# The first input's parts made straight from PSUM, its squares summed as loaded, and a 128-byte buffer below the weights

## The chip, the cores and the metric

The kernel runs on one core of one Trainium2 chip. The metric is the time of one execution on the device in microseconds; before the change the median of three runs is 2146.05 us (2145.6 to 2146.09).

## The reference

Four layers over one sequence of 256 tokens with 1024 features, all in float32. Each layer adds half of a SwiGLU feed-forward network (FFN), a token mixer, and half of a second FFN:

```python
for layer in range(DEPTH):                                   # 4
    h = h + 0.5 * swiglu(rmsnorm(h, ffn_norm[layer, 0]), ffn_w_gate_up[layer, 0], ffn_w_down[layer, 0])
    hn = rmsnorm(h, mixer_norm[layer])                       # mixer: gated DeltaNet, short convolution,
    h = h + mix(hn)                                          # sparse attention, gated DeltaNet
    h = h + 0.5 * swiglu(rmsnorm(h, ffn_norm[layer, 1]), ffn_w_gate_up[layer, 1], ffn_w_down[layer, 1])
rmsnorm(x, w) = x * rsqrt(mean(x * x) + 1e-6) * w
swiglu(h, gu, dn): g, u = split(h @ gu); (silu(g) * u) @ dn   # 1024 -> 2 x 2816 -> 1024
```

## The kernel before

**Parts.** Every float32 operand of a large product is split in two: `hi`, the value rounded to the float32r format that TensorE (PE) takes, and `lo`, what the rounding left. A product is three matmuls, hi by hi, lo by hi and hi by lo (`mm3`, lines 335 to 337). The activations are kept transposed, features on partitions, and are the moving operand of 256 columns (`xhi`, `xlo`, and later `hhi`, `hlo`); a block of 128 by 128 of a weight's part is the stationary one. In a few places (the last down projection, `last_rows`, lines 418 to 420, and the `add_wide` pieces of the mixers, lines 1433 to 1435 and 1983 to 1986) it is the other way round: the weights' part moves with 512 columns.

**Weights.** `Weights` streams them through four `raw` buffers of 8 KB per partition. SP issues the loads. `hi()` makes a half buffer's high part on ScalarE (ACT) or VectorE (DVE), `lo()` the low part on DVE, into six buffers each of `whi` and `wlo` of 4 KB. Where a stage has room, parts go into lent `b8` buffers instead (`wboth`). A piece of 48 matmuls takes two halves.

**Addresses.** Buffers are stacked in each partition's memory in the order of their pools (const, big, work, raw, parts), at multiples of 32 bytes. In the built program all `b8` buffers (activations' parts and lent parts) begin at 224 modulo 256 bytes, and `raw`, `whi` and `wlo` at 160; rows and blocks inside them are whole multiples of 512 bytes long, so that every moving operand and stationary block named above begins at those residues too.

**The start.** x is loaded with tokens on partitions (`xin`), in two halves of 512 features, and then the first weights, of which the first `raw` buffer in quarters. PE transposes x into PSUM; DVE copies it to `x`, ACT makes `xhi` with the norm's weight as a scale, DVE makes `xlo`, POOL (GpSimd) squares it. The sums of the squares over the features are matmuls with one column (`norm_sums`, line 315). The first piece's matmuls are written so that parts which come late are used late (`first_cols`, `late_cols`). The row factor of the norm is only applied behind the products (`norm_rows`, `rb`). Fillers (`busy`) keep PE at work while it waits for x.

**Order.** Everything is issued in the order in which the code is written; a planner sets the order inside the mixers. Each engine takes its own instructions in that order and waits on semaphores.

Of the kernel before, what the change touches and what calls it, by code (L numbers as in the profile page):

```python
# [7 lines left out]
F32 = mybir.dt.float32  # L8
# [3 lines left out]
AF = mybir.ActivationFunctionType  # L12
OP = mybir.AluOpType
AX = mybir.AxisListType

D = 1024
S = 256
DFF = 2816
KT = D // 128
FT = DFF // 128  # L20
EPS = 1e-6
# [9 lines left out]
class Weights:  # L31
# [45 lines left out]
    def view(t, dims):  # L77
# [3 lines left out]
        names = "abc"[:len(dims)]  # L81
        return t[:, :n].rearrange(f"p ({' '.join(names)}) -> p {' '.join(names)}", **dict(zip(names, dims)))

    def load(self):
        while not self.hold and self.loaded < min(self.freed + self.LOADS, len(self.srcs)):
            src = self.srcs[self.loaded]
            raw = self.view(self.raw_pool.tile([128, 2048], F32, name="raw"), src.shape[1:])
            if len(src.shape) == 4:

                n = src.shape[3] // (1 if self.loaded else 2)  # L90
                for c in range(0, src.shape[3], n):
                    for b in range(src.shape[2]):
                        self.nc.sync.dma_start(raw[:, :, b, c:c + n], src[:, :, b, c:c + n])
            else:
                self.nc.sync.dma_start(raw, src)
            self.raw[self.loaded] = raw
            if self.plan:
                self.plan.set(("raw", self.loaded), 5.0)
            self.loaded += 1
# [72 lines left out]
def kernel(ctx, tc, plan, a, out):  # L172
    nc = tc.nc
# [3 lines left out]
    work = ctx.enter_context(tc.tile_pool(name="work", bufs=2))  # L177
    psum = ctx.enter_context(tc.tile_pool(name="psum", bufs=1, space=bass.MemoryType.PSUM))
    W = Weights(tc, ctx)

    def bank(tag="acc"):
        return psum.tile([128, 512], F32, name=tag, tag=tag, bufs=4)

    def mid():
        return bank("mid")

    def b8(dt, name, shape=(KT, S)):
        return big.tile([128, *shape], dt, name=name, tag="b8", bufs=10)
# [3 lines left out]
    def t2(name, shape=(2, S), dt=F32):  # L192
        return work.tile([128, *shape], dt, name=name, tag="t2", bufs=8)
# [35 lines left out]
    for kind, layer, i in plan:  # L229
        if kind == "ffn":  # L230
            steps.append((add_pairs(a["ffn_w_gate_up"][layer, i]), add_rows(a["ffn_w_down"][layer, i], DFF)))
        if kind == "gdn":
            w = a["gdn_w_in"][i]
            units = {}
            for u in GDN_ORDER:
                c = D * "qkvg".index(u[0]) + 512 * int(u[1])
                units[u] = (add_wide if u[0] == "g" else add_cols)(w, *([c] if u[0] == "g" else [c, 512]))
            steps.append((units, add_rows(a["gdn_w_out"][i], D)))
        if kind == "nsa":
            w = a["nsa_w_in"][i]  # L240
# [4 lines left out]
        if kind == "sc":  # L245
            w = a["sc_w_in"][i]
# [3 lines left out]
    xin = b8(F32, "xin", (2, D))  # L250
    norm_rows = t2("norm_rows", (128,))[:96]
    nc.sync.dma_start(norm_rows[:64], a["ffn_norm"].rearrange("l i (k p) -> (l i k) p", p=128))
    nc.scalar.dma_start(norm_rows[64:], a["mixer_norm"].rearrange("l (k p) -> (l k) p", p=128))
    for c in range(0, D, 512):
        nc.sync.dma_start(xin[:, :, c:c + 512], a["x"][0, :, c:c + 512].rearrange("(t p) d -> p t d", p=128))
    W.load()


    ij = const.tile([128, 128], I32, name="ij")
# [3 lines left out]
    ones = const.tile([128, 128], F32, name="ones")  # L263
# [1 line left out]
    neghalf = const.tile([128, 16], F32, name="neghalf")  # L265
    nc.vector.memset(neghalf, -0.5)

    def busy(times):

        p = mid()  # L270
        for _ in range(times):
            nc.tensor.matmul(p[:, :128], ones, ident, start=True, stop=True)


    x = const.tile([128, KT, S], F32, name="x")
    busy(5)
    p = bank()
    nc.tensor.transpose(p[:, :96], norm_rows, ident[:96, :96])
    norms = const.tile([128, 96], F32, name="norms")
    nc.vector.tensor_copy(norms, p[:, :96])  # L280

    class Normed:
        pass


    def norm_start():
        n = Normed()
        n.hi, n.lo = b8(F32R, "xhi"), b8(F32R, "xlo")
        n.sq = b8(F32, "sq")
        return n  # L290

    def norm_hi(n, k, col, squares=True):
        for kk in (k, k + 1):
            nc.scalar.activation(n.hi[:, kk], x[:, kk], AF.Copy, scale=norms[:, col + kk:col + kk + 1])  # L294
        if squares:
            norm_square(n, k)

    def norm_square(n, k):
        nc.scalar.activation(n.sq[:, k:k + 2], x[:, k:k + 2], AF.Square)

    def norm_lo(n, k, col):
        for kk in (k, k + 1):
            nc.vector.scalar_tensor_tensor(n.lo[:, kk], x[:, kk], norms[:, col + kk:col + kk + 1], n.hi[:, kk],
                                           op0=OP.mult, op1=OP.subtract)

    def norm_squares(n, k):

        nc.vector.tensor_add(n.sq[:, :2], n.sq[:, :2], n.sq[:, k:k + 2])

    def norm_sums(n):  # L310

        p = bank()
        for t in range(2):
            for k in range(2):
                nc.tensor.matmul(p[:, t:t + 1], n.sq[:, k, t * 128:(t + 1) * 128], ones[:, :1], start=k == 0,
                                 stop=k == 1)
        n.r = work.tile([128, 2], F32, name="rcol")
        yield
        nc.vector.tensor_scalar(n.r, p[:, :2], 1.0 / D, EPS, op0=OP.mult, op1=OP.add)  # L319
        yield  # L320
        nc.gpsimd.tensor_tensor(n.r, n.r, neghalf[:, :2], op=OP.pow)  # L321

    def norm_rows(n):

        dg = t2("dg", (2, 128))
        for t in range(2):
            nc.vector.tensor_scalar(dg[:, t], ident, n.r[:, t:t + 1], None, op0=OP.mult)
        p = bank()[:, :S]
        nc.tensor.matmul(p, ones, dg, start=True, stop=True)
        W.lo()  # L330
        n.rb = work.tile([128, S], F32, name="rb")
        nc.vector.tensor_copy(n.rb, p)
# [6 lines left out]
    def pair(tag="acc"):  # L339
        return bank(tag).rearrange("p (s t) -> p s t", s=2)  # L340

    def rest(steps):

        while True:
            try:
                next(steps)
            except StopIteration as end:
                return end.value

    def add_rows_steps(pieces, inputs, ktiles, scale, next_col, engine=None, planned=False):  # L350
# [3 lines left out]
        for q, j in enumerate(pieces):  # L354
# [3 lines left out]
            if last:  # L358
                nn = norm_start()
# [74 lines left out]
    def first_cols(j, acc, ks, n):  # L434

        parts = [[v.rearrange("p (s c) -> p s c", s=2) if len(v.shape) == 2 else v for v in W.part(j, k)] for k in ks]
        for k, (hi, lo) in zip(ks, parts):
            for s in range(2):
                for x in (n.hi, n.lo):
                    nc.tensor.matmul(acc[:, s], hi[:, s], x[:, k], start=k == 0 and s == 0 and x is n.hi, stop=False,  # L440
                                     skip_group_check=True)
        for k, (hi, lo) in zip(ks, parts):
            for s in range(2):
                nc.tensor.matmul(acc[:, s], lo[:, s], n.hi[:, k], start=False, stop=False, skip_group_check=True)

    def two_cols(j, acc, ks, n):

# [21 lines left out]
    def dense(j, n, first=False):  # L469
        acc = pair()  # L470
        W.use(j)
        if j == 0:
            first_cols(j, acc, range(4), n)
        else:
            (late_cols if first else two_cols)(j, acc, range(4), n)
        (late_cols if first else two_cols)(j, acc, range(4, KT), n)
        W.retire(j)
        return acc

    def two_first(pieces, n):  # L480

        accs = [dense(pieces[0], n, True), pair()]
        W.use(pieces[1])
        for k in range(KT):
            if k == 2:
                rest(norm_sums(n))
                W.hi()
                W.hi()
            if k == 5:
                norm_rows(n)  # L490
                W.ahead(pieces[0] + 3)
            two_cols(pieces[1], accs[1], [k], n)
        W.retire(pieces[1])
        W.ahead(pieces[1] + 3)
        return accs
# [1563 lines left out]
    cols = []  # L2059
    for kind, layer, i in plan:  # L2060
        cols.append((layer * 2 + i) * 8 if kind == "ffn" else 64 + layer * 8)
    cols.append(None)
    n = norm_start()
    busy(4)
    for k in range(0, KT, 2):
        if k == 4:
            busy(4)
        p = bank().rearrange("p (k t) -> p k t", k=2)
        for kk in range(2):
            for t in range(2):  # L2070
                nc.tensor.transpose(p[:, kk, t * 128:(t + 1) * 128],
                                    xin[:, t, (k + kk) * 128:(k + kk + 1) * 128], ident)
        nc.vector.tensor_copy(x[:, k:k + 2], p)
        norm_hi(n, k, cols[0], False)
        nc.gpsimd.tensor_mul(n.sq[:, k:k + 2], x[:, k:k + 2], x[:, k:k + 2])
        if k == 2:
            W.hi()
        if k:
            norm_lo(n, k - 2, cols[0])
        if k == 6:  # L2080
            W.lo()
    norm_lo(n, KT - 2, cols[0])
    W.ahead(0)
    W.hi()
    W.hi()
    W.lo()
    for k in range(2, KT, 2):
        norm_squares(n, k)
    W.ahead(1)
    def loads_of(kind, i):  # L2090
        return gdn_loads(g, i) if kind == "gdn" else nsa_loads(g, i) if kind == "nsa" else iter(())

# [2 lines left out]
    for q, (kind, layer, i) in enumerate(plan):  # L2095
        if kind == "ffn":
            then = (plan[q + 1:q + 2] or plan[:1])[0]
            n = ffn(steps[q], n, cols[q + 1], loads_of(then[0], then[2]), dict(gdn=SPARE, nsa=min(SPARE, 3)).get(then[0], 0))
        if kind == "gdn":
            n = gdn(steps[q], n, cols[q + 1], g)  # L2100
        if kind == "nsa":
            n = nsa(steps[q], n, cols[q + 1], g)
        if kind == "sc":
            n = sc(steps[q], n, cols[q + 1])
# [42 lines left out]
```

## Time and profile before

| | |
|---|---|
| median of three runs | 2146.05 us |
| the profiled execution | 2144.0 us, of which the span of its instructions 2142.2 us |
| PE busy | 2119.2 us, 99% |
| PE loading weights (PEld) | 2065.6 us, 96% |
| DVE, ACT, POOL busy | 66%, 50%, 13% |
| granted TensorE clock, mean | 0.998 of full |

Matmuls are pipelined and their recorded durations overlap, so that the pace of a stretch is read from the starts: the start of the last less that of the first, over the number of matmuls between them. In the names `out<-in`, `acc` and `mid` are PSUM banks. PE at the start, before about 28 us, is where it waits for others; behind that it is given work almost without a gap.

### The profile page before, as it was taken

How to read it: one execution, taken by the hardware profiler on the slowest of the kernel's cores; microseconds unless marked ns; L12 is line 12 of the kernel's file. 1: busy time of each engine (PE TensorE's matmuls, PEld its weight loads, DVE VectorE, ACT ScalarE, POOL GpSimd, SP SyncE). 2: the span in 40 equal slices, each digit the busy share in tenths (PEclk: the TensorE clock that was granted, in tenths of full speed). 3: DMA queues.
4: the chain of work that ended last, by engine and by line, in shares of the span. 5: the costliest groups of instructions: out<-in, count | busy, mean ns of one | idle time of the engine just before them, and what ended most of it. 6: DMA issues, size and time to landing. Idle time of an engine off the chain costs nothing. (4 is left out here: it accounts for less than half of the span.)

```text
span 2142.2 us, 41781 instructions
## 1 busy us (share of the span) xinstructions
PE 2119.2 (99%) x17335; PEld 2065.6 (96%) x17335; DVE 1407.0 (66%) x2322; ACT 1066.0 (50%) x1800; POOL 283.7 (13%) x312
## 2 busy tenths in 40 slices
PE   8999999999999999999999998999999999999999
PEld 8999999999999999999999987899999999999997
DVE  7664897665566476665666468876556648986653
ACT  5453754544454355444555445654445436655542
POOL 2110101121021010210121010011102201011210
PEclk9999999999999999999999999999999999999999
DMA  8564451556565555655566443155546562524652
GB/s 246 185 242 138 140 181 40 177 178 211 157 204 189 186 167 188 194 182 196 165 200 230 145 162 119 55 187 184 192 157 200 197 236 89 168 85 138 198 196 80
DMA packets 263790, 363.22 MB, mean 170 GB/s; under 512 B 17856, under 2 KB 211520, under 8 KB 263600
## 3 DMA queue, kind: packets, MB, share of 16 engines
q1 hardware_dynamic: 257520, 357.11, 50.6%
q8 instruction: 136, 2.23, 0.4%
q10 hardware_dynamic: 5136, 2.12, 0.4%
q0 software_dynamic: 944, 1.33, 0.3%
q14 instruction: 54, 0.44, 0.1%
HBM read 357.89 MB, written 2.10 MB: 168 GB/s over the span
## 5 line engine op out<-in xcount | busy, mean ns | idle before, releaser
L136 DVE TENSOR_TENSOR wlo<-raw,whi 128x1024 fp32r<-128x1024 f32 x640 | 775.4, 1219 | 234.6 <-ACT whi L126 234.2
L335 PE MATMUL acc<-xhi,whi 128*128 128x256 f32 x3248 | 911.7, 281 | 0.0
L337 PE MATMUL acc<-xhi,wlo 128*128 128x256 f32 x3248 | 909.1, 280 | 0.0
L336 PE MATMUL acc<-xlo,whi 128*128 128x256 f32 x3248 | 907.6, 279 | 0.0
L126 ACT ACTIVATE whi<-raw 128x1024 fp32r<-128x1024 f32 x633 | 660.2, 1050 | 352.1 <-PE mid L336 204.1
L336 PEld LDWEIGHTS acc<-xlo,whi 128*128 128x128 f32 x3248 | 610.7, 188 | 0.5
L337 PEld LDWEIGHTS acc<-xhi,wlo 128*128 128x128 f32 x3248 | 609.7, 188 | 0.0
L335 PEld LDWEIGHTS acc<-xhi,whi 128*128 128x128 f32 x3248 | 608.9, 187 | 0.5
L510 POOL TENSOR_TENSOR t_h<-t_gate,rb 128x256 f32<-128x256 f32 x176 | 197.8, 1124 | 740.9 <-ACT t_gate L506 735.7
L337 PE MATMUL mid<-hhi,wlo 128*128 128x256 f32 x1056 | 295.1, 279 | 0.0
L336 PE MATMUL mid<-hlo,whi 128*128 128x256 f32 x1056 | 294.4, 279 | 0.0
L335 PE MATMUL mid<-hhi,whi 128*128 128x256 f32 x1056 | 294.4, 279 | 0.0
L506 ACT ACTIVATE t_gate<-t_gate 128x256 f32<-128x256 f32 x176 | 73.6, 418 | 311.0 <-DVE t_gate L505 311.0
L505 DVE TENSOR_TENSOR t_gate<-acc,rb 128x256 f32<-128x256 f32 x176 | 74.5, 423 | 189.3 <-PE acc L337 189.3
L336 PEld LDWEIGHTS mid<-hlo,whi 128*128 128x128 f32 x1056 | 198.6, 188 | 0.0
L337 PEld LDWEIGHTS mid<-hhi,wlo 128*128 128x128 f32 x1056 | 198.3, 188 | 0.0
L335 PEld LDWEIGHTS mid<-hhi,whi 128*128 128x128 f32 x1056 | 197.9, 187 | 0.0
L512 DVE TENSOR_TENSOR t_h<-acc,t_h 128x256 f32<-128x256 f32 x176 | 74.8, 425 | 128.7 <-POOL t_h L510 128.7
L517 ACT ACTIVATE hhi<-t_h 128x256 fp32r<-128x256 f32 x176 | 73.7, 419 | 152.1 <-DVE t_h L512 152.1
L321 POOL TENSOR_TENSOR rcol<-rcol,neghalf 128x2 f32<-128x2 f32 x12 | 8.4, 704 | 654.4 <-DVE rcol L319 654.4
L519 DVE TENSOR_TENSOR hlo<-t_h,hhi 128x256 fp32r<-128x256 f32 x176 | 74.0, 420 | 7.7 <-ACT hhi L517 7.7
L294 ACT ACTIVATE xhi<-x,norms 128x256 fp32r<-128x256 f32 x96 | 43.2, 498 | 48.5 <-DVE x L368 42.2
(437 smaller groups left out, 2591.5 us busy)
## 6 DMA issues: line engine op xcount, KB each, us to landing
raw<-in_ffn_w_gate_up_dram SPq DMA_DIRECT2D x350, 512.0 KB, 5.3
raw<-in_ffn_w_down_dram SPq DMA_DIRECT2D x88, 1024.0 KB, 5.0
raw<-in_gdn_w_in_dram SPq DMA_DIRECT2D x32, 1024.0 KB, 5.4
raw<-in_nsa_w_in_dram SPq DMA_DIRECT2D x10, 1024.0 KB, 5.1
raw<-in_gdn_w_out_dram SPq DMA_DIRECT2D x8, 1024.0 KB, 5.1
raw<-in_sc_w_in_dram SPq DMA_DIRECT2D x16, 512.0 KB, 4.7
raw<-in_sc_w_in_dram SPq DMA_DIRECT2D x4, 1024.0 KB, 6.0
raw<-in_sc_w_out_dram SPq DMA_DIRECT2D x4, 1024.0 KB, 5.7
```

The source lines that it names most:

```text
L126: self.nc.scalar.activation(self.parts[g][0], raw, AF.Copy)
L136: (engine or self.nc.vector).tensor_sub(self.parts[g][1], self.half(g), self.parts[g][0])
L294: nc.scalar.activation(n.hi[:, kk], x[:, kk], AF.Copy, scale=norms[:, col + kk:col + kk + 1])
L335: nc.tensor.matmul(o, w[0], x[0], start=first, stop=False, skip_group_check=True)
L336: nc.tensor.matmul(o, w[0], x[1], start=False, stop=False, skip_group_check=True)
L337: nc.tensor.matmul(o, w[1], x[0], start=False, stop=last, skip_group_check=True)
L505: nc.vector.tensor_mul(t, acc[:, 0], n.rb)
L506: nc.scalar.activation(s, t, AF.Silu)
L510: nc.gpsimd.tensor_mul(sr, s, n.rb)
L512: nc.vector.tensor_mul(h, acc[:, 1], sr)
L517: nc.scalar.activation(hi, h, AF.Copy)
L519: nc.vector.tensor_sub(lo, h, hi)
```

## The change

The transposes of x now go to `mid` banks, and the parts are made straight from there: ACT makes `xhi` and DVE `xlo` from PSUM, without the copy to `x` before. The copies to `x` (needed for the residual) are made by ACT later, inside the second piece of the first FFN. The squares are taken of `xin` as it was loaded, tokens on partitions, by ACT, which adds them up along the features as it goes (`accum_out`); so the sum over features needs no matmul, only an addition of two halves on DVE. The `sq` buffer isn't used for the first norm. The two pairs of sums stand in a new buffer `xsums` of 2 x 16 float32 values, 128 bytes, in the pool that lies below `raw` and the parts: these now begin at 32 modulo 256 bytes instead of 160, everything in `big` stays at 224.

SP loads x and the first two `raw` buffers in another order: the quarter-columns that the first piece needs come first. The first `whi` is made on DVE. The first piece uses one order for both halves of the features: all hi by hi, all lo by hi, all hi by lo. The row factor is formed one step later (`k == 6`).

```diff
+    def first(self, inputs):
+        srcs = self.srcs[:2]
+        raw = [self.view(self.raw_pool.tile([128, 2048], F32, name="raw"), x.shape[1:]) for x in srcs]
+        n = srcs[0].shape[3] // 2
+        for c in range(2):
+            for x in range(2):
+                if c == 0:
+                    self.nc.sync.dma_start(*inputs[x])
+                for b in range(2):
+                    self.nc.sync.dma_start(raw[x][:, :, b, c * n:c * n + n], srcs[x][:, :, b, c * n:c * n + n])
...
     def norm_sums(n):
...
+            sums = n.r
         yield
-        nc.vector.tensor_scalar(n.r, p[:, :2], 1.0 / D, EPS, op0=OP.mult, op1=OP.add)
+        if n.sums:
+            nc.vector.tensor_add(n.r, *n.sums)
+        nc.vector.tensor_scalar(n.r, sums, 1.0 / D, EPS, op0=OP.mult, op1=OP.add)
...
     def first_cols(j, acc, ks, n):
...
+        for w, x in ((0, n.hi), (0, n.lo), (1, n.hi)):
+            for k, both in zip(ks, parts):
+                for s in range(2):
+                    nc.tensor.matmul(acc[:, s], both[w][:, s], x[:, k], start=k == 0 and s == 0 and not w and x is n.hi,
+                                     stop=w == 1 and k == KT - 1, skip_group_check=True)
...
             if k == 2:
-                rest(norm_sums(n))
+                if n.sums is None:
+                    rest(norm_sums(n))
                 W.hi()
                 W.hi()
-            if k == 5:
+                if n.sums:
+                    n.copies()
+            if k == (5 if n.sums is None else 6):
                 norm_rows(n)
...
-        nc.vector.tensor_copy(x[:, k:k + 2], p)
-        norm_hi(n, k, cols[0], False)
-        nc.gpsimd.tensor_mul(n.sq[:, k:k + 2], x[:, k:k + 2], x[:, k:k + 2])
...
+    sums = work.tile([128, 2, 16], F32, name="xsums", bufs=1)
+    n.sums = [sums[:, h, :2] for h in range(2)]
...
+        for kk in range(2):
+            c = cols[0] + k + kk
+            nc.scalar.activation(n.hi[:, k + kk], p[:, kk], AF.Copy, scale=norms[:, c:c + 1])
...
+            nc.vector.scalar_tensor_tensor(n.lo[:, k + kk], ps[k][:, kk], norms[:, c:c + 1], n.hi[:, k + kk],
+                                           op0=OP.mult, op1=OP.subtract)
...
+            nc.scalar.activation(t2("xsq"), xin[:, t, 512 * h:512 * h + 512].rearrange("p (k c) -> p k c", k=2),
+                                 AF.Square, accum_out=n.sums[h][:, t:t + 1])
...
+    busy(4, "acc")
+    ps = {k: turned(k) for k in (0, 2)}
+    W.hi("V")
+    remains(0)
+    remains(2)
+    W.lo()
+    square_sums(0)
+    W.hi()
+    busy(4, "acc")
+    for k in (4, 6):
+        ps[k] = turned(k)
+        remains(k)
+    W.lo()
     W.hi()
     W.hi()
+    square_sums(1)
     W.ahead(1)
+    rest(norm_sums(n))
+
+    def copies():
+        for k in ps:
+            nc.scalar.activation(x[:, k:k + 2], ps[k], AF.Copy)
```

How the instructions move, at three places of the start; the names are tiles, the figures partitions by elements, xN a run of equal ones. First the loads that SP issues, before:

```order
L252 DMA norm_rows<-in_ffn_norm_dram 64x128
L255 DMA xin<-in_x_dram 128x2x512 x2
L93 DMA raw<-in_ffn_w_gate_up_dram 128x4x128 x4
L93 DMA raw<-in_ffn_w_gate_up_dram 128x4x256 x42
L95 DMA raw<-in_ffn_w_down_dram 128x2x1024 x11
```

and now:

```order
L264 DMA norm_rows<-in_ffn_norm_dram 64x128
L92 DMA xin<-in_x_dram 128x2x512
L94 DMA raw<-in_ffn_w_gate_up_dram 128x4x128 x2
L92 DMA xin<-in_x_dram 128x2x512
L94 DMA raw<-in_ffn_w_gate_up_dram 128x4x128 x6
L105 DMA raw<-in_ffn_w_gate_up_dram 128x4x256 x40
```

Two quarter loads of weights stand ahead of the second half of x, and the second buffer's first quarters ahead of the first buffer's last ones.

Then ACT from its first table load to the first gate of the FFN, before:

```order
L294 ACT_TABLE_LOAD
L294 ACTIVATE xhi<-x,norms 128x256 x4
L126 ACTIVATE whi<-raw 128x1024
L294 ACTIVATE xhi<-x,norms 128x256 x4
L126 ACTIVATE whi<-raw 128x1024 x9
```

and now (`xsq` is a scratch buffer that nobody reads):

```order
L2094 ACT_TABLE_LOAD
L2094 ACTIVATE xhi<-mid,norms 128x256 x4
L2105 ACTIVATE xsq,xsums<-xin 128x512 x2
L138 ACTIVATE whi<-raw 128x1024
L2094 ACTIVATE xhi<-mid,norms 128x256 x4
L138 ACTIVATE whi<-raw 128x1024 x2
L2105 ACTIVATE xsq,xsums<-xin 128x512 x2
L138 ACTIVATE whi<-raw 128x1024 x2
L2129 ACTIVATE x<-mid 128x512 x4
L138 ACTIVATE whi<-raw 128x1024 x4
```

Squares and copies of x have come to ACT, and one whi has left it.

Last DVE, from the copy of the norms on, before:

```order
L280 COPY norms<-acc 128x96
L2073 COPY x<-acc 128x512 x2
L303 SCALAR_TENSOR_TENSOR xlo<-x,norms,xhi 128x256 x2
L2073 COPY x<-acc 128x512
L303 SCALAR_TENSOR_TENSOR xlo<-x,norms,xhi 128x256 x2
L2073 COPY x<-acc 128x512
L303 SCALAR_TENSOR_TENSOR xlo<-x,norms,xhi 128x256 x2
L136 TENSOR_TENSOR wlo<-raw,whi 128x1024
L303 SCALAR_TENSOR_TENSOR xlo<-x,norms,xhi 128x256 x2
L136 TENSOR_TENSOR wlo<-raw,whi 128x1024 x2
L308 TENSOR_TENSOR sq<-sq 128x512 x3
L136 TENSOR_TENSOR wlo<-raw,whi 128x1024
```

and now:

```order
L291 COPY norms<-acc 128x96
L140 CAST whi<-raw 128x1024
L2100 SCALAR_TENSOR_TENSOR xlo<-mid,norms,xhi 128x256 x4
L148 TENSOR_TENSOR wlo<-raw,whi 128x1024
L2100 SCALAR_TENSOR_TENSOR xlo<-mid,norms,xhi 128x256 x4
L148 TENSOR_TENSOR wlo<-raw,whi 128x1024 x3
L338 TENSOR_TENSOR rcol<-xsums 128x2
L339 TENSOR_SCALAR rcol<-rcol 128x2
```

The four copies and three additions are gone, the first whi is here, and the first wlo stands ahead of the second four remainders.

## Rows read from the trace of the kernel before

**Rows 1.** Page, part 1: busy time, share of the span and instructions of TensorE.
```profile
PE 2119.2 (99%) x17335; PEld 2065.6 (96%) x17335; DVE 1407.0 (66%) x2322; ACT 1066.0 (50%) x1800; POOL 283.7 (13%) x312
```

**Rows 2.** Groups by line, tile and shape, TensorE: count, busy us, mean ns, idle.
```profile
L335 PE MATMUL acc<-xhi,whi 128*128 128x256 f32 x3248 | 911.7, 281 | 0.0
...
L335 PE MATMUL mid<-hhi,whi 128*128 128x256 f32 x1056 | 294.4, 279 | 0.0
...
L465 PE MATMUL acc<-xhi,whi 128*128 128x256 f32 x168 | 42.8, 284 | 0.0
...
L335 PE MATMUL acc<-gzh,whi 128*128 128x256 f32 x128 | 36.3, 283 | 0.0
...
L418 PE MATMUL mid<-whi,hhi 128*128 128x512 f32 x88 | 34.7, 394 | 0.0
...
L1983 PE MATMUL acc<-whi,xhi 128*128 128x512 f32 x56 | 22.7, 406 | 0.0
...
L335 PE MATMUL acc<-nzh,whi 128*128 128x256 f32 x64 | 19.3, 302 | 0.0
...
L1433 PE MATMUL acc<-whi,xhi 128*128 128x512 f32 x48 | 19.3, 403 | 0.0
...
L335 PE MATMUL mid<-sc_zh,whi 128*128 128x256 f32 x64 | 17.9, 279 | 0.0
```

**Rows 3.** Timeline (start us, us taken), FFN: first and last of 29.
```profile
99.96 0.28 PE L335 MATMUL acc<-xhi,whi 128*128 128x256 f32 x1
...
109.85 0.28 PE L335 MATMUL acc<-xhi,whi 128*128 128x256 f32 x1
```

**Rows 4.** Timeline, down projection with lent parts: first and last of 16.
```profile
185.95 0.28 PE L335 MATMUL mid<-hhi,wboth 128*128 128x256 f32 x1
...
191.35 0.28 PE L335 MATMUL mid<-hhi,wboth 128*128 128x256 f32 x1
```

**Rows 5.** Timeline, own parts right behind lent ones: first and last of 32.
```profile
175.07 0.28 PE L335 MATMUL mid<-hhi,whi 128*128 128x256 f32 x1
...
185.61 0.28 PE L335 MATMUL mid<-hhi,whi 128*128 128x256 f32 x1
```

**Rows 6.** Timeline, last down projection, 512 columns: first and last of 20.
```profile
2098.10 0.39 PE L418 MATMUL mid<-whi,hhi 128*128 128x512 f32 x1
...
2111.40 0.39 PE L418 MATMUL mid<-whi,hhi 128*128 128x512 f32 x1
```

**Rows 7.** Timeline, 512 columns of lent parts moving: first and last of 6.
```profile
226.69 0.39 PE L1433 MATMUL acc<-wboth,xhi 128*128 128x512 f32 x1
...
227.83 0.39 PE L1435 MATMUL acc<-wboth,xlo 128*128 128x512 f32 x1
```

**Rows 8.** Timeline of the start, all engines; in brackets the idle time before.
```profile
5.80 0.86 PEld L2071 LDWEIGHTS acc<-ident,xin 128*128 128x128 f32 x8 [0.33 <-DMA xin<-in_x_dram]
...
7.23 1.71 ACT L294 ACTIVATE xhi<-x,norms 128x256 fp32r<-128x256 f32 x4 [4.76 <-DVE x L2073]
...
10.17 0.19 PEld L440 LDWEIGHTS acc<-xhi,whi 128*128 128x128 f32 x1 [1.74 <-ACT whi L126]
...
13.80 4.08 ACT L126 ACTIVATE whi<-raw 128x1024 fp32r<-128x1024 f32 x4 [0.30 <-DMA raw<-in_ffn_w_gate_up_dram]
...
15.31 1.97 PE L444 MATMUL acc<-xhi,wlo 128*128 128x256 f32 x8 [2.69 <-DVE wlo L136]
...
20.78 0.28 PE L335 MATMUL acc<-xhi,whi 128*128 128x256 f32 x1
...
22.19 0.95 PE L315 MATMUL acc<-ones,sq 128*128 128x1 f32 x8
...
25.45 1.06 ACT L126 ACTIVATE whi<-raw 128x1024 fp32r<-128x1024 f32 x1 [2.75 <-PE acc L337]
```

**Rows 9.** Windows: PE, PEld, DVE, ACT, POOL busy us (count), clock, DMA share, GB/s.
```profile
15.30:18.90 3.60, 3.58 (x17) 3.54 (x17) 3.60 (x5) 2.50 (x3) 0.00 (x0) 0.53 1.08 340
```

**Rows 10.** Groups of DVE up to 30 us: the low parts.
```profile
L136 DVE TENSOR_TENSOR wlo<-raw,whi 128x1024 fp32r<-128x1024 f32 x9 | 10.6, 1217 | 0.0
```

More of the change, by code (lines that the diff above doesn't have):

```diff
@@ L82, in view @@
         return t[:, :n].rearrange(f"p ({' '.join(names)}) -> p {' '.join(names)}", **dict(zip(names, dims)))
+    def first(self, inputs):
[8 more added lines that the diff above has]
+                    self.nc.sync.dma_start(raw[x][:, :, b, c * n:c * n + n], srcs[x][:, :, b, c * n:c * n + n])
+        self.raw.update(enumerate(raw))
+        self.loaded = 2
+        self.load()
     def load(self):
@@ L88, in load @@
             if len(src.shape) == 4:
[L90 to L93, printed above, removed]
+                for b in range(src.shape[2]):
+                    self.nc.sync.dma_start(raw[:, :, b], src[:, :, b])
             else:
@@ L253 @@
     nc.scalar.dma_start(norm_rows[64:], a["mixer_norm"].rearrange("l (k p) -> (l k) p", p=128))
-    for c in range(0, D, 512):
-        nc.sync.dma_start(xin[:, :, c:c + 512], a["x"][0, :, c:c + 512].rearrange("(t p) d -> p t d", p=128))
-    W.load()
+    W.first([(xin[:, :, c:c + 512], a["x"][0, :, c:c + 512].rearrange("(t p) d -> p t d", p=128))
+             for c in range(0, D, 512)])
     ij = const.tile([128, 128], I32, name="ij")
@@ L266, with busy @@
     nc.vector.memset(neghalf, -0.5)
-    def busy(times):
-        p = mid()
+    def busy(times, tag="mid"):
+        p = bank(tag)
         for _ in range(times):
@@ L282, with norm_start @@
     class Normed:
-        pass
-    def norm_start():
+        sums = None
+    def norm_start(squares=True):
         n = Normed()
         n.hi, n.lo = b8(F32R, "xhi"), b8(F32R, "xlo")
-        n.sq = b8(F32, "sq")
+        if squares:
+            n.sq = b8(F32, "sq")
         return n
@@ L310, in norm_sums @@
     def norm_sums(n):
[L312 to L316, printed above, removed]
-        n.r = work.tile([128, 2], F32, name="rcol")
+        n.r = work.tile([128, 2], F32, name="rcol")
+        if n.sums is None:
+            p = bank()
+            for t in range(2):
+                for k in range(2):
+                    nc.tensor.matmul(p[:, t:t + 1], n.sq[:, k, t * 128:(t + 1) * 128], ones[:, :1], start=k == 0,
+                                     stop=k == 1)
+            sums = p[:, :2]
+        else:
+            sums = n.r
         yield
-        nc.vector.tensor_scalar(n.r, p[:, :2], 1.0 / D, EPS, op0=OP.mult, op1=OP.add)
+        if n.sums:
+            nc.vector.tensor_add(n.r, *n.sums)
+        nc.vector.tensor_scalar(n.r, sums, 1.0 / D, EPS, op0=OP.mult, op1=OP.add)
         yield
@@ L436, in first_cols @@
         parts = [[v.rearrange("p (s c) -> p s c", s=2) if len(v.shape) == 2 else v for v in W.part(j, k)] for k in ks]
[L437 to L444, printed above, removed]
+        for w, x in ((0, n.hi), (0, n.lo), (1, n.hi)):
[3 more added lines that the diff above has]
+                                     stop=w == 1 and k == KT - 1, skip_group_check=True)
     def two_cols(j, acc, ks, n):
@@ L471, in dense @@
         W.use(j)
[L472 to L476, printed above, removed]
+        f = first_cols if j == 0 else late_cols if first else two_cols
+        f(j, acc, range(4), n)
+        f(j, acc, range(4, KT), n)
         W.retire(j)
@@ L485, in two_first @@
             if k == 2:
-                rest(norm_sums(n))
+                if n.sums is None:
+                    rest(norm_sums(n))
                 W.hi()
                 W.hi()
-            if k == 5:
+                if n.sums:
+                    n.copies()
+            if k == (5 if n.sums is None else 6):
                 norm_rows(n)
@@ L2062, with turned @@
     cols.append(None)
[L2063 to L2068, printed above, removed]
+    n = norm_start(False)
+    sums = work.tile([128, 2, 16], F32, name="xsums", bufs=1)
+    n.sums = [sums[:, h, :2] for h in range(2)]
+    def turned(k):
+        p = mid().rearrange("p (k t) -> p k t", k=2)
         for kk in range(2):
@@ L2072, with remains, square_sums @@
                                     xin[:, t, (k + kk) * 128:(k + kk + 1) * 128], ident)
-        nc.vector.tensor_copy(x[:, k:k + 2], p)
-        norm_hi(n, k, cols[0], False)
-        nc.gpsimd.tensor_mul(n.sq[:, k:k + 2], x[:, k:k + 2], x[:, k:k + 2])
[L2076 to L2083, printed above, removed]
+        for kk in range(2):
+            c = cols[0] + k + kk
+            nc.scalar.activation(n.hi[:, k + kk], p[:, kk], AF.Copy, scale=norms[:, c:c + 1])
+        return p
+    def remains(k):
+        for kk in range(2):
+            c = cols[0] + k + kk
+            nc.vector.scalar_tensor_tensor(n.lo[:, k + kk], ps[k][:, kk], norms[:, c:c + 1], n.hi[:, k + kk],
+                                           op0=OP.mult, op1=OP.subtract)
+    def square_sums(h):
+        for t in range(2):
+            nc.scalar.activation(t2("xsq"), xin[:, t, 512 * h:512 * h + 512].rearrange("p (k c) -> p k c", k=2),
[13 more added lines that the diff above has]
+    W.lo()
     W.hi()
     W.hi()
-    W.lo()
-    for k in range(2, KT, 2):
-        norm_squares(n, k)
+    square_sums(1)
     W.ahead(1)
+    rest(norm_sums(n))
+    def copies():
+        for k in ps:
+            nc.scalar.activation(x[:, k:k + 2], ps[k], AF.Copy)
+    n.copies = copies
     def loads_of(kind, i):
```

## The prediction

> **What bounds the kernel now.** First the page's busy table [rows 1]: TensorE (PE) is busy 99% of a 2142.2 us span, and behind the start no wait of any weight shows; the order of instructions behind the first two pieces is the same in both kernels, buffer numbers apart. So outside the first 28 us the time can change only through the pace of the matmuls themselves. Second, which matmuls these are [rows 2]: the groups that take a weights' part (whi or wlo) as the stationary block, with 256 columns moving, are six groups of 3248, 1056, 168, 128, 64 and 64, each standing three times (hi by hi, lo by hi, hi by lo): 4728 x 3 = 14,184 matmuls. A further 88 + 48 + 56 = 192, times three = 576, use the parts the other way round, as 512 moving columns. Third, their pace, from first and last of a stretch with their count, because the recorded durations of pipelined matmuls overlap:
> - ordinary FFN columns, parts at 160 modulo 256 and the moving activations at 224: 29 of line 335 from 99.96 to 109.85, so 9.89 us for 84 matmuls, 117.7 ns each [rows 3].
> - the same line with lent parts ("wboth", in b8 buffers at 224 modulo 256): 15 x 3 matmuls in 5.40 us, 120.0 ns [rows 4].
> - own parts right behind lent ones: 31 x 3 in 10.54 us, 113.3 ns [rows 5]. The two ways of running at the same addresses last until the next interruption; nearly all of the kernel has 117.7.
> - the last down projection, parts (160) moving with 512 columns, hidden values (224) as weights: 19 x 3 in 13.30 us, 233.3 ns [rows 6].
> - 512 columns with lent parts moving, both at 224: 5 in 1.14 us, 228 ns [rows 7].
>
> The pace thus differs with nothing changed but where the operands lie. I read these numbers as steps of 6.67 ns, 64 bytes of moving operand each: 1024 bytes that begin 32 bytes into such a step touch 17 of them, and 17 x 6.67 = 113.3; 2048 bytes touch 33, 220.0. Then the rows say how many steps a matmul loses while the next block of weights is loaded. Call offset the start of the weights less that of the moving operand, modulo 256. Offset 0: 18 steps (120.0) with 256 columns and about 34 (228) with 512: one lost both times. Offset -64 (own parts as weights): 17.66 steps, two thirds lost, or none in the stretches at 113.3. Offset +64 (last projection): 35 steps, two lost. This counting is my reading, not a thing that a row states.
>
> **The change, part by part.**
> *The address.* The new buffer is 128 bytes and lies below raw and the parts, so these move from 160 to 32 modulo 256, while activations stay at 224. The offset of the 14,184 becomes 32 - 224 = -192, which is +64: that of the last projection now. The 576 go to -64. If only the offset counts, a matmul of 256 columns takes 17 + 2 = 19 steps, 126.7 ns, 9.0 more than 117.7; I take 8.9, as stretches near 120 remain at changes of stage. 14,184 x 8.9 ns = +126 us. The 576 go from 233.3 to 33.67 steps, 224.4: 576 x 8.9 = -5 us. The trace has no matmul with weights at 32 against columns at 224, so the price is bounded by the nearest rows: 113.3 (no step lost; 14,184 x -4.4 = -62 us) and 126.7 (two lost, as at the same offset). I take the upper one since it is the only row with that offset.
>
> [...]
>
> *The start.* All on PE's path until the second piece is done.
> Removed: the wait of 2.69 us before line 444 (for wlo, behind the copies and remainders of x on DVE) [rows 8]. [...] The sums on PE, eight matmuls of one column at line 315: 0.95 as recorded [rows 8], some 0.8 without the overlap of the last. DVE loses four copies and three additions of 512 columns, POOL four products; nobody but the removed wait waited for them last.
> Moved and added: SP puts two quarter loads (256 KB each) ahead of the second half of x. At 340 GB/s [rows 9] that is 1.5 us. The first half is turned at 5.80 [rows 8], half a megabyte later makes 7.3, so the second is there near 8.8 and, with 1.0 us of transposes, dense work starts at about 9.8 instead of 10.17. ACT: four xhi at 0.43 from 6.5 to 8.2, two squares of 512 columns (half of whi's 4.08 / 4 = 1.02 us [rows 8], so 0.5 each) to 9.3, whi of the second tile when 2 MB are in: the third megabyte was in at 13.80, when the second whi could begin [rows 8], 3 us a megabyte, so 10.8 to 11.9; the other four xhi wait behind it and end near 13.6. DVE has the first whi (no more than ACT's 1.02), eight remainders (as large as xhi, 1.71 / 4 = 0.43 each [rows 8]) and wlo (1217 ns [rows 10]); the second wlo ends near 15.3, and the last eight matmuls of the first piece near 16.3 instead of 20.78 [rows 8]. With 0.8 for the sums and 0.3 of a new wait on the third wlo the second piece ends 5 us earlier. The four copies of x (512 columns like the squares, 0.5 each, 2.0 in all) are queued on ACT ahead of the whi of the third piece; ACT waited 2.75 us for PE there [rows 8], which covers them; without that cover they cost up to 2.0. [...] Both ends: -5.5 and -1; I take -4.5, nearer the sum than the mishaps.
>
> *Sum* against the profiled execution, 2144.0 us (span 2142.2 and 1.8 around it): 2144.0 + 126 - 5 - 4.5 = 2260.5; the median of the runs stands 2.05 above that execution, so 2262. Some short stretches may fall into the state without losses, as now; I forecast 2260.
>
> **Rivals.**
> A. The address doesn't count, or counts modulo 128 (160 and 32 are the same there, and so are the offsets -64 and +64): the pace stays 117.7 and only the start remains, 2146 - 4.5 = 2141.5. For it: the homes seen so far differ by only 2.3 ns a matmul, and of 160 against 32 no row tells anything directly. Against: under modulo 128 the last projection should lose as little per load as the FFN, and it loses two steps against two thirds.
> B. The other side: at 32 the load of the weights falls between the moving reads and the state of rows 5 (17 steps, none lost) becomes the usual one. Place: all FFN columns; price 14,184 x 4.4 = -62 us, so 2079. With the rest at two lost steps it outweighs them from two thirds of the matmuls on (8.9 against 4.4 + 8.9). For it: the same addresses already run in two ways, so what a matmul loses hangs on when the load begins, not on the offset alone. Against: in the trace that state follows lent parts and doesn't outlast an interruption.
> C. One step is lost, as for lent parts: 120.0, 14,184 x 2.3 = +32, 2174. For it: 120.0 is the commonest number apart from 117.7. Against: it belongs to offset 0.
>
> **How the numbers follow.** Forecast (two steps lost) 0.64, with its own range 2235 to 2275 (from 7 ns to 9.5 ns a matmul); C 0.10; A 0.12; B 0.14. What a measurement of this kernel can tell from no change is about 0.2%, 4.3 us; A's 2141.5 lies at that edge, so its 0.12 goes half to faster, half to no change. Faster 0.14 + 0.06 = 0.20, no change 0.06, slower 0.74. The range takes in forecast, C and A, with a start that gains up to 8: 2138 to 2275, leaving out B and a start of the tail, less than 0.2.
>
> **What would show it.** In the FFN at 100 us, the line that is now 335: 27 in 10 us instead of 29 if two steps are lost, 28 or 29 for C and A, 30 for B; lent parts unchanged at 120.0; the last projection near 224 ns. At the start: dense work at about 9.8, no stretch at the low clock before 20 us, the second piece from about 16.5, no matmul with one column in the first FFN. The forecast is wrong if own parts run at 120 or less; its cause is wrong if they are slow while the 512-column matmuls are no faster.

## The result and the profile after

The changed kernel takes 2088.45 us (median of four runs, 2087.93 to 2088.84) against 2145.82 of the kernel before, a ratio of 0.9736 with a 95% interval from 0.9724 to 0.9747. It is faster by 57.4 us where 114 us more were forecast. Rival B is what happened: the pace of 113.3 ns, a rare one before, is the usual one now.

PE is as busy as before, in a span that is 55.2 us shorter. The page's busy table, of the kernel after, PE and PEld first:

```profile
PE 2065.2 (99%) x17327; PEld 2012.6 (96%) x17327; DVE 1398.7 (67%) x2317; ACT 1070.2 (51%) x1811; POOL 277.0 (13%) x308
```

So the matmuls follow each other faster. The timeline of PE after (start, time taken, line), first and last of 31 matmuls of the high by high line in the stretch of [rows 3]:

```profile
99.65 0.28 PE L355 MATMUL acc<-xhi,whi 128*128 128x256 f32 x1
...
109.85 0.28 PE L355 MATMUL acc<-xhi,whi 128*128 128x256 f32 x1
```

10.20 us for 30 x 3 matmuls are 113.3 ns each, where [rows 3] had 117.7. The recorded 0.28 us of one matmul reads the same in both (279 to 280 ns before and 276 after, in the mean by line, from 100 to 110 us), far more than either pace: the starts tell it. Lent parts, first and last of 16 of the same line after:

```profile
176.06 0.28 PE L355 MATMUL mid<-hhi,wboth 128*128 128x256 f32 x1
...
181.47 0.28 PE L355 MATMUL mid<-hhi,wboth 128*128 128x256 f32 x1
```

5.41 us for 15 x 3: 120.2, which is the 120.0 of [rows 4] as far as rows with two decimals tell; the lent parts and the activations stayed where they were. Own parts right behind lent ones, first and last of 31:

```profile
164.76 0.28 PE L355 MATMUL mid<-hhi,whi 128*128 128x256 f32 x1
...
175.36 0.28 PE L355 MATMUL mid<-hhi,whi 128*128 128x256 f32 x1
```

10.60 us for 30 x 3: 117.8. That is [rows 5] in a mirror. The kernel before has 117.7 nearly everywhere and 113.3 behind most stretches with lent parts; the kernel after has 113.3 nearly everywhere and 117.8 behind lent parts. (117.7 and 117.8 are one pace, 117.77 where a longer stretch is counted.) The same pair of paces occurs at both places of the parts, and which of the two is usual has changed sides.

In the last down projection three lines in a row, and the first again, show an uneven step:

```profile
2041.64 0.39 PE L438 MATMUL mid<-whi,hhi 128*128 128x512 f32 x1
2041.87 0.39 PE L439 MATMUL mid<-wlo,hhi 128*128 128x512 f32 x1
2042.10 0.39 PE L440 MATMUL mid<-whi,hlo 128*128 128x512 f32 x1
2042.33 0.39 PE L438 MATMUL mid<-whi,hhi 128*128 128x512 f32 x1
```

0.69 us for three; by line the steps are 226, 229 and 232 ns in the median, and 228.9 in the mean over all 263, where [rows 6] had 233.3.

The start, as the timeline of all engines after has it:

```profile
5.72 0.86 PEld L2090 LDWEIGHTS mid<-ident,xin 128*128 128x128 f32 x8 [0.18 <-DMA xin<-in_x_dram]
...
8.88 0.86 PEld L2090 LDWEIGHTS mid<-ident,xin 128*128 128x128 f32 x8 [1.36 <-DMA xin<-in_x_dram]
...
9.71 1.00 PEld L460 LDWEIGHTS acc<-xhi,whi 128*128 128x128 f32 x8
...
10.71 1.06 ACT L138 ACTIVATE whi<-raw 128x1024 fp32r<-128x1024 f32 x1 [1.51 <-DMA raw<-in_ffn_w_gate_up_dram]
11.68 1.55 ACT L2094 ACTIVATE xhi<-mid,norms 128x256 fp32r<-128x256 f32 x4
...
15.38 1.20 PE L460 MATMUL acc<-xhi,wlo 128*128 128x256 f32 x8 [0.63 <-DVE wlo L148]
...
16.41 0.28 PE L355 MATMUL acc<-xhi,whi 128*128 128x256 f32 x1
...
17.51 0.15 DVE L338 TENSOR_TENSOR rcol<-xsums 128x2 f32<-128x2 f32 x1
...
21.86 1.06 ACT L138 ACTIVATE whi<-raw 128x1024 fp32r<-128x1024 f32 x1 [3.47 <-DMA raw<-in_ffn_w_gate_up_dram]
22.82 2.04 ACT L2129 ACTIVATE x<-mid 128x512 f32<-128x512 f32 x4
...
24.73 4.04 ACT L138 ACTIVATE whi<-raw 128x1024 fp32r<-128x1024 f32 x4
```

and its windows (PE, PEld, DVE, ACT, POOL busy, granted clock, DMA share, GB/s):

```profile
1.50:9.70 8.20, 7.00 (x42) 6.63 (x43) 2.41 (x6) 4.07 (x9) 0.00 (x0) 1.00 0.90 260
9.70:16.40 6.70, 6.07 (x51) 5.80 (x50) 5.11 (x9) 5.55 (x10) 0.00 (x0) 1.00 1.14 314
16.40:22.00 5.60, 5.60 (x50) 5.55 (x49) 3.48 (x8) 1.41 (x4) 0.70 (x1) 1.00 1.09 348
```

Dense work begins at 9.71, PE's wait for wlo has shrunk from 2.69 [rows 8] to 0.63, the granted clock is 1.00 in all three windows, and the second piece begins at 16.41.

Matching the last 17,200 matmuls one to one, from start to start in the two profiled executions, gives where the 55.2 us of the span are:

| part | change, us |
|---|---|
| start, to 20.5 us of the new kernel | -5.6 |
| 256 columns with own parts, 14,040 matmuls | -49.5 |
| from such a stretch to the next work, 86 times | +2.0 |
| 512 columns with own parts moving, 554 | -2.2 |
| everything else (lent parts next to nothing) | +0.2 |

### The profile page after: what moved, and what is told of

The parts are those of the page before. It is cut to its first block, busy times and chain, and to the rows that moved or that the text cites. A ratio compares the mean times of both kernels' runs of the same rounds, so it can differ in the third digit from the quotient of the medians.

```text
span 2087.0 us, 41769 instructions
## 1 busy us (share of the span) xinstructions
PE 2065.2 (99%) x17327; PEld 2012.6 (96%) x17327; DVE 1398.7 (67%) x2317; ACT 1070.2 (51%) x1811; POOL 277.0 (13%) x308
## 5 line engine op out<-in xcount | busy, mean ns | idle before, releaser
L355 PE MATMUL acc<-xhi,whi 128*128 128x256 f32 x3248 | 902.3, 278 | 0.0
L357 PE MATMUL acc<-xhi,wlo 128*128 128x256 f32 x3248 | 898.0, 276 | 0.0
L356 PE MATMUL acc<-xlo,whi 128*128 128x256 f32 x3248 | 898.0, 276 | 0.0
```

Source lines behind the costliest of these rows:

```text
L355: nc.tensor.matmul(o, w[0], x[0], start=first, stop=False, skip_group_check=True)
L356: nc.tensor.matmul(o, w[0], x[1], start=False, stop=False, skip_group_check=True)
L357: nc.tensor.matmul(o, w[1], x[0], start=False, stop=last, skip_group_check=True)
```

## The experiments

Two theories stood at first. P: the place of the parts decides which pace is the usual one. H: the new start leaves PE in the other pace, which then goes on, and the place counts for nothing. H was a serious one, as both paces occur at both places. "Distance" below is the start of the weights' parts less that of the moving activations, modulo 256: 192 before, 64 after. Where the text says a single run, there is one time and one profile; the runs of one kernel lie up to 2.2 us apart.

**The parts alone.**

```diff
         self.part_pool = ctx.enter_context(tc.tile_pool(name="parts", bufs=self.ROOM))
+        self.nc.gpsimd.memset(self.part_pool.tile([128, 32], F32, name="pad", bufs=1), 0)
```

> The kernel before with 128 unused bytes below whi and wlo: only the parts move, from 160 to 32 modulo 256; raw, activations, start and order stay. Theory P (the place of the parts decides which of two paces, 113.3 or 117.7 ns a matmul, is the usual one): own parts at 113.3 in most of the FFN, about 50 us less, 2096; the stretches behind lent parts at 117.7 instead of 113.3. Theory H (the new start leaves PE in the other pace and the place counts for nothing): 117.7 stays, 2146.

Measured: 2093.14 us against 2144.88, ratio 0.9758 (0.9744 to 0.9773), so -51.7. The same line, first and last of 31 in the timeline of PE:

```profile
99.67 0.28 PE L336 MATMUL acc<-xhi,whi 128*128 128x256 f32 x1
...
109.87 0.28 PE L336 MATMUL acc<-xhi,whi 128*128 128x256 f32 x1
```

10.20 / 90 = 113.3. P holds and H falls: 128 bytes that nobody reads, with raw, the order and the start as before, make nine tenths of the gain.

**The start alone.** The sums' buffer of the changed kernel is doubled, so that the parts stand at 160 again:

```diff
-    sums = work.tile([128, 2, 16], F32, name="xsums", bufs=1)
+    sums = work.tile([128, 2, 32], F32, name="xsums", bufs=1)
```

> The changed kernel with sums of 256 bytes instead of 128, so the parts stand at 160 again; the start is the new one. P: the usual pace is 117.7, only the start's gain of about 5.5 us stays, 2140. H: 113.3 stays, 2088.

Measured: 2139.82 against 2144.88, ratio 0.9975 (0.9965 to 0.9986): -5.1. The timeline of PE, first and last of 29:

```profile
99.96 0.28 PE L355 MATMUL acc<-xhi,whi 128*128 128x256 f32 x1
...
109.85 0.28 PE L355 MATMUL acc<-xhi,whi 128*128 128x256 f32 x1
```

9.89 / 84 = 117.7, the old pace, under the new start. The two halves, -51.7 and -5.1, add up to -56.8 of the -57.4 measured together.

**Distance or address.** In the kernel before, unused bytes below everything move activations, raw and parts together; first 128:

```diff
     const = ctx.enter_context(tc.tile_pool(name="const", bufs=1))
+    nc.gpsimd.memset(const.tile([128, 32], F32, name="pad"), 0)
```

> The kernel before with 128 unused bytes below everything: parts at 32, activations at 96, so that weights less moving operand is -64 modulo 256 as before. P, if the distance between the two counts: 117.7, 2146. P, if the weights' own address counts: 113.3, 2096. H: 2146.

Measured: 2146.03, a single run. The timeline of PE, first and last of 29:

```profile
99.91 0.28 PE L336 MATMUL acc<-xhi,whi 128*128 128x256 f32 x1
...
109.80 0.28 PE L336 MATMUL acc<-xhi,whi 128*128 128x256 f32 x1
```

9.89 / 84 = 117.7 with the parts at 32, where they ran at 113.3 against activations at 224. So it isn't the address of the weights: with the distance back at 192 the old pace is back. Nor is it the added memset, which is in this run too.

**Steps of 64 bytes.** The same with `[128, 8]`, 32 bytes, in the kernel before and in the changed one: now the moving operand begins on a multiple of 64.

> The kernel before with 32 unused bytes below everything: distance -64 as before, but the moving operand begins at 0 modulo 256, on a multiple of 64. If a matmul reads in steps of 64 bytes, 1024 bytes now touch 16 of them and not 17: between 113.3 (one step lost: 14,184 x -4.4 = -62, 2084) and the 111.6 of the shortest matmuls seen (-86, 2060). If only the distance counts: 117.7, 2146.

Measured: 2144.46, a single run. First and last of 30 in the timeline of PE:

```profile
99.73 0.28 PE L336 MATMUL acc<-xhi,whi 128*128 128x256 f32 x1
...
109.98 0.28 PE L336 MATMUL acc<-xhi,whi 128*128 128x256 f32 x1
```

10.25 / 87 = 117.8, the pace of the kernel before.

> The changed kernel with 32 unused bytes below everything: activations at 0, parts at 64, distance 64. If the 113.3 ns of this distance are 17 steps of 64 bytes because the moving operand begins inside a step, it is now 16, and the next limit is the 111.6 of the shortest spacing seen: 14,184 x -1.7 = -24, 2064. If only the distance counts: 2088.

Measured: 2087.59, a single run. First and last of 30 in the timeline of PE:

```profile
99.84 0.28 PE L356 MATMUL acc<-xhi,whi 128*128 128x256 f32 x1
...
109.70 0.28 PE L356 MATMUL acc<-xhi,whi 128*128 128x256 f32 x1
```

9.86 / 87 = 113.3. Neither kernel gained from an operand that begins on a step, so the prediction's count of 17 touched steps, of which an operand that begins on a step would have saved one, is refuted. With parts and activations moved together the pace stayed at distance 192 (twice) and at 64 (here).

**All distances.** Unused bytes in the parts' pool of the changed kernel, as in the first experiment, with 8, 16, 24, 40, 48, 56 and 64 elements in place of 32:

> The changed kernel with whi and wlo (raw not) 32 bytes higher, at 64; distance 96 (weights less moving operand, modulo 256). The step found so far is that the distance decides: 113.3 ns at 64, 117.7 at 192. Theory S (what counts is how far the load's reads are from the matmul's reads within 256 bytes, 128 is best): 113.3 or less, 2088 or below. Theory L (several paces, the usual one picked without such an order): 113.3, 117.7 or 120, so 2088, 2140 or 2166. Steps of 64 bytes: the same as at 64, 2088.

> Parts 64 bytes higher, at 96; distance 128. S: the best of all, between 111.6 (the shortest spacing seen, 14,184 x -1.7 = -24, 2064) and 113.3 (2088). L: any of 2088, 2140, 2166.

> Parts 96 bytes higher, at 128; distance 160, between 128 (about 119) and 192 (117.8): 2140 to 2155.

> Parts 160 bytes higher, at 192; distance 224, 32 bytes short of 0. S: between 117.7 at 192 and 120 at 0, 2140 to 2166. Steps of 64 bytes: as at 192, 2140.

> Parts 192 bytes higher, at 224 like the lent ones; distance 0. As the lent parts run at 120.0: 14,184 x 6.7 = +95 of the changed kernel, less what is lost at interruptions anyway, about 2175.

> Parts 224 bytes higher, at 0; distance 32. L (paces between 113.3 and 120 without an order by distance; so far 64: 113.3, 96: about 118, 128: about 119, 192: 117.8, 224: about 116.8): 2088 to 2166. If the spread around 64 is even on both sides, it is like 96: 2151.

> Parts 256 bytes higher, at 32 as in the changed kernel; distance 64 modulo 256, but 256 bytes more modulo 512. If the period is 256: 2088. If it is 512 or more: another pace, 2140 or more.

Measured, a single run each, beside the kernels that have a distance of 64 and 192 with the same start (medians). The paces are worked out from the starts: the median over the stretches of 84 matmuls with own parts and 256 columns that have no pause, and for 512 columns the mean of the last down projection, where the operands have changed roles, so that the distance is the negative one.

| distance | time, us | 256 columns, ns | distance in the last projection | 512 columns, ns |
|---|---|---|---|---|
| 0 | 2169.51 | 120.0 | 0 | 226.8 |
| 32 | 2149.42 | 118.3 | 224 | 233.3 |
| 64, the changed kernel | 2088.45 | 113.3 | 192 | 228.9 |
| 96 | 2150.66 | 118.6 | 160 | 233.3 |
| 128 | 2154.16 | 118.6 | 128 | 232.4 |
| 160 | 2172.22 | 120.0 | 96 | 234.3 |
| 192, sums of 256 bytes | 2139.82 | 117.8 | 64 | 233.3 |
| 224 | 2128.31 | 116.7 | 32 | 233.3 |

256 bytes more (distance 64 again) took 2087.84, with 113.3 ns: so a period of 256 fits, and one of 128 does not, as 64 and 192 differ. The slow end, as the timeline of PE shows it for distance 160, first and last of 29:

```profile
99.75 0.28 PE L356 MATMUL acc<-xhi,whi 128*128 128x256 f32 x1
...
109.83 0.28 PE L356 MATMUL acc<-xhi,whi 128*128 128x256 f32 x1
```

10.08 / 84 = 120.0. Theory S (far apart is good, 128 is best) fell with distances 96 and 128, and theory L's list of three times missed both: 2150.66 and 2154.16 lie between 2140 and 2166. The expectations that were taken from neighbouring distances did no better: 32 was met, 0 came 5 us below, 160 lies 17 us above its range and 224 some 12 us below. Neighbours 32 bytes apart say little about each other. No version here beats the changed kernel: the fastest, 2087.59 and 2087.84, lie 0.9 and 0.6 us below its median, which a single run each can't tell from nothing.

## Why the prediction was wrong

**What bounds the kernel** was right: nothing but the pace of the matmuls and the start has moved, and the six groups of [rows 2] carry it.

**The step that failed is the price at distance 64.** It read "two lost, as at the same offset" from the 512-column matmuls of [rows 6] and put it on the 256-column ones of [rows 2]: 126.7 ns and +126 us. At that distance the 256-column matmuls took 113.3 ns, and the own parts gave -49.5 us. No experiment has a stretch of 84 matmuls with 256 columns slower than 120.1. The table shows why the transfer doesn't hold: distance 64 is the best for 256 columns and among the slowest for 512, and distance 0 is the best for 512 and among the slowest for 256. Nor does 233.3 ns mark distance 64: in the table it stands at four of the eight distances. What a distance costs belongs to the shape of the matmul, or to which operand is which; the two changed together in [rows 6], and the runs don't part them. Under the price lay the counting of steps, which was called a reading; two kernels with another alignment refuted it. What makes 64 the fast distance, the runs leave open.

**Rival B** had the place, the sign and the price of a matmul (113.3) right, at 0.14, and was left outside the range. Its price for the whole was 14,184 x 4.4 = 62; the own parts gave 49.5. The rest is counted from the trace: in windows of six matmuls 12,108 of the changed kernel run at 113.3 where 534 did before, so 11,574 x 4.45 = 51.5, and 1344 still run at 117.7: 582 of these right behind lent parts, 384 behind pieces of 512 columns, 186 in one stretch of the last FFN that begins behind a pause of 0.2 us, the rest in short stretches. About 2.5 us went into pauses: steps of over 150 ns rose from 66 to 91. One such place is the first piece of the third FFN, in the timeline of the changed kernel (PE and DVE):

```profile
555.93 1.67 DVE L317 SCALAR_TENSOR_TENSOR xlo<-x,norms,xhi 128x256 fp32r<-128x256 f32 x4
...
556.79 1.38 PE L482 MATMUL acc<-xlo,whi 128*128 128x256 f32 x8
```

and in that of the kernel before:

```profile
572.62 1.67 DVE L303 SCALAR_TENSOR_TENSOR xlo<-x,norms,xhi 128x256 fp32r<-128x256 f32 x4
...
573.76 1.10 PE L465 MATMUL acc<-xlo,whi 128*128 128x256 f32 x8
```

The faster PE asks for xlo 0.86 us behind the start of the four remainders instead of 1.14, and the last four of its eight matmuls then start 0.18 to 0.23 us apart, behind remainders that DVE starts 0.40 apart, instead of 0.12: 0.28 us longer in all. B's reason, that the load falls between the moving reads, is not shown by any run: in the two traces a load is recorded 1 to 5 ns behind the start of a matmul, in stretches at 113.3 and at 117.7 alike.

**Rival A and modulo 128** fell: 32 and 160 differ by 52 us in the first experiment. Nor is the address free: 128 unused bytes moved the pace from 117.7 to 113.3 ns, and the eight distances show 113.3 to 120.0 for one instruction stream.

**The 576 matmuls with 512 columns** were forecast at 224.4 ns and -5 us; they came to 228.9 in the last projection and -2.2 in all. The sign was right, the size half.

**The start** was right step by step: dense work at 9.71 (forecast 9.8), xhi's second four at 11.68 to 13.23 (11.9 to 13.6), the second piece from 16.41 (16.3 for the last of the first), a granted clock of 1.00 in all windows to 22 us, the four copies of x 2.04 us long (2.0), with no pause of PE behind them before 40 us. Behind the copies ACT goes on without a wait, where it had waited 2.75 us for PE [rows 8], so the cover was there as forecast. The gain is 5.6 us in the two traces and 4.9 in that of the start alone; between medians it is 5.1 at the old place of the parts and 4.7 at the new one (2093.14 against 2088.45), where 4.5 was taken and -5.5 was the far bound. What the two bounds, -5.5 and -1, count for a lowered clock at the start is shown by no run by itself; the granted clock was 0.53 in the window of [rows 9] and is 1.00 in the three windows here.

**The chances.** The trace had one pace on each side of 117.7 for 256 columns, 113.3 and 120.0, and no row with 256 columns at distance 64. From there a range from all at 113.3 (2079) to all at 126.7 was what the bounds allowed. The prediction had named both ends and then cut off the lower one.

## What to carry to other kernels

In this kernel, with float32r, one load per matmul and PE busy 99% of the span, a buffer of 32 to 224 bytes that lies below one operand and not below the other put the time anywhere between 2088 and 2172 us. For a kernel like it, compute the start of the stationary operand less that of the moving one, modulo 256, for both kernels before reading anything else into a changed time. Scan the eight multiples of 32 with unused bytes; here the result could neither be interpolated nor carried from one shape of matmul to another. To see it, divide the time from start to start by the count; the recorded time of a matmul, 0.28 us here at 113.3 ns, at 117.7 and at 120.0, hides it.

## What the runs showed of the hardware

With float32r operands, 256 columns moving and a load of 128 columns per matmul, the usual spacing lies between 113.3 and 120.0 ns at a granted clock of 0.998, and the distance modulo 256 decides which. That the addresses themselves count for nothing was run at distances 64 and 192; at the other six only the parts were moved. One of the eight multiples of 32 is better than the next best by 3.4 ns a matmul, which is 40 us here (2088.45 against 2128.31). The distance alone doesn't fix the pace of every stretch: at 64 and 192 the same two paces occur, 113.3 and 117.8, and the one that a stretch begins with mostly goes on until the next interruption: of the unbroken stretches of 25 and more matmuls with own parts and 256 columns, read in windows of six, all 42 of the kernel before kept theirs, and 31 of 43 of the changed kernel; the other 12 went over to 113.3 within their first seven steps. Two of these, from 228.5 and 1757.4 us, began at about 117.5 and went over at one step of 122 ns. At 96, 128 and 224 some stretches of 84 keep a second pace too: 117.3, 120.0 and 117.8. What makes a stretch take one or the other, why 64 is the good one, and whether a distance between multiples of 32 is better still, stays open: the pools place buffers at multiples of 32. Lent parts at distance 64, which would concern the 528 matmuls at 120.0 and the 582 right behind them, were not tried.
